# Three kinds of SBUF pools give back their space tile by tile instead of pool by pool

## The chip, the cores and the metric

The kernel runs on one core of one Trainium2 chip. The metric is the device time of one execution in microseconds (us); the median of three runs is given. Beside it stands one profiled execution with its own time, from which all rows of the trace are taken.

The engines are called PE (TensorE, matmul), DVE (VectorE), ACT (ScalarE), POOL (GpSimd) and SP (SyncE, which here only issues loads and stores). DMAs are issued on three queues: SP's, ACT's and POOL's.

## What is computed

Two layers of a transformer over 512 latent tokens and 256 context tokens of width 1024, all in float32. Layer 0 mixes tokens by neighbourhood attention (8 heads) beside a spatial gating unit (SGU), layer 1 by retention (8 heads). Each is followed by a gated MLP with a depthwise convolution (ConvFFN). Around every part stand RMS norms, and shift, scale and gate come from a conditioning vector through `ada_w`. Only the latent stream is put out.

```python
for i in range(DEPTH):                      # DEPTH = 2
    sh1, sc1, g1, sh2, sc2, g2 = jnp.split(silu(c) @ ada_w[i] + ada_b[i], 6)
    h_lat = modulate(rmsnorm(x, norm_g[i, 0]), sh1, sc1)
    h_ctx = modulate(rmsnorm(xc, norm_g[i, 0]), csh1, csc1)
    y = hybrid_na_sgu(h_ctx, h_lat, ...) if i % 2 == 0 else retention_mixer(h_ctx, h_lat, ...)
    x = x + g1 * rmsnorm(y_lat, norm_g[i, 1])
    h = modulate(rmsnorm(x, norm_g[i, 2]), sh2, sc2)
    x = x + g2 * rmsnorm(conv_ffn(h, ...), norm_g[i, 3])
    # in layer 0 the context stream xc goes the same way, with csh, csc, cg
```

## The kernel before

The work stands as one stream of instructions for each engine, which a tile framework records from the Python program; it assigns addresses to tiles and adds the semaphore waits that the tiles' uses demand. Within an engine the order is that of the program; engines run apart and meet only at waits. One helper (L71) records every operation of PE, DVE and ACT, so rows of the trace are told apart by the names of tiles, not by lines.

A float32 product is made of three matmuls of a split operand: ACT writes the high part, DVE the low part (`split`, L110). So every weight is loaded by SP into one of three `raw` buffers, split by ACT and then by DVE, and used by PE. A `raw` buffer is free again when DVE has done its part.

There are five phases one after the other, and each opens its own pool of SBUF space with `phase` (L138): `sguw` (the SGU), `attp` (attention), `ffnp0` (the first ConvFFN), `retp` (retention) and `ffnp1` (the second ConvFFN). Inside the SGU two more are opened: `firstp` for the first norms (L751) and `sgup` (L791), which takes over `firstp`'s space. A phase's pool lies where the one before it lay. `lay` (L145) fixes the place of each tag in a pool. The pools that live through the whole program (`cp`, `bp`, `lp`, and those in PSUM and DRAM) are opened elsewhere.

Since a phase's tiles lie on those of the phase before, the first instructions that write them must wait for the old uses. In the kernel before, the framework lets a pool's space go as a whole: the first write into the new pool on an engine waits for the last uses, by every engine and DMA queue, of all tiles of the old pool.

What else the prediction names:

- Attention adds bias tiles to its scores. `load_slab` (L988) loads a strip of the bias table with a DMA on POOL's queue, `bias_tiles` (L993) scales it on POOL (L998) and adds it to `mask` (L1003 to L1005), which SP loads at the phase's start. POOL also copies one half of `kb` (L970), the low part of the keys, which PE reads in `s<-kb,q`.
- `ada_half` (L251) works out the gates and scales in small steps between the other work: a memset of `acc` on POOL (L257), a row load into it (L258), four loads of `ar`, and multiply-adds of `ar` into `acc` on DVE. The steps stand at fixed places of the program.
- `mx` and `wsg` are products of the SGU on PE, `wsg` its last ones.
- At each phase's end the residual of every token tile is stored to DRAM from ACT's queue (`xd`, L390), normed and transposed on PE (`ht`, `htc`), scaled into `sa` and `sb` (or `hc`) and split into `hb` (or `h0c`, `h1c`) for the next phase.
- In a ConvFFN `wp` and `wpm` are the first two blocks' weights, `pf` their products, `cw` the convolution's weights, `f0..`, `f1..` and `fo..` weights of later blocks, `pre`, `cv`, `b12` and `blk` work tiles.
- In retention `rv` holds the values, `rn` is their product in PSUM, `dist`, `cos`, `sin`, `dec` and `gng` are tables, `rwv`, `rwg`, `rwk` and `wx` weights, `rkc` and `rq` products.

Of the kernel before, what the change touches and what calls it, by code (L numbers as in the profile page):

```python
# [78 lines left out]
class Trunk:  # L79
# [56 lines left out]
        return self.place(i, name, at)  # L136

    def phase(self, ctx, name, extra, wide=2048):  # L138
        self.xp = ctx.enter_context(self.tc.tile_pool(name=name, bufs=1))
        self.extra = extra  # L140
        self.wide = wide
        self.turn = 0
        return self.xp
# [581 lines left out]
    def sgu(self, y, xn):  # L725
        S, V, T, G, a = self.S, self.V, self.T, self.G, self.a
        toks = (4, 5, 0, 1, 2, 3)
        with ExitStack() as ctx:
# [5 lines left out]
            def ug_units(which, js):  # L734
                return [
                    self.unit(
                        a["hyb_ug"][(which * 4 + i) * P : (which * 4 + i + 1) * P], f"ug{which}{i}", at=0 if which else Q3
                    )
                    for i in js
                ]  # L740

            def ug(ps, t, w, ks, cs=slice(0, 512)):
                hc = self.hcols(t)
                for k in ks:
                    c = slice((k % 2) * 512 + cs.start, (k % 2) * 512 + cs.stop)
                    wk = w[k // 2 % len(w)]
                    self.mm3(ps, hc(k), (wk[0][:, c], wk[1][:, c]), k == 0, k == KD - 1)

            ps = {}
            with ExitStack() as c2:  # L750
                fp = c2.enter_context(self.tc.tile_pool(name="firstp", bufs=1))  # L751
                cs = self.cs
                c4 = fp.tile([P, KD, 4], F32R, name="c4", tag="c4")
                for s in range(2):
                    S.activation(c4[:, :, 2 * s], cs[:, 8 * s : 8 * s + 8], AF.Copy)
                    V.tensor_tensor(
                        out=c4[:, :, 2 * s + 1],
                        in0=cs[:, 8 * s : 8 * s + 8],
                        in1=c4[:, :, 2 * s].bitcast(F32),
                        op=ALU.subtract,  # L760
                    )
                self.c4 = c4
                self.alloc_h("a")
                xT = {}
                ada = self.ada_first(0, fp, True, "C")
                chunks = ((2, (4, 5)), (0, (0, 1)), (1, (2, 3)))
                for n, (chunk, ct) in enumerate(chunks):
                    if n:
                        self.first_load(ct, xn)
                    self.first_x(ct, xn)  # L770
                    for _ in range((1, 2, 5)[n]):
                        next(ada, None)
                    self.first_xT(chunk, ct, xn, fp, xT)
                for _ in ada:
                    pass
                for q in range(4):
                    w = ug_units(1, (q,))
                    for chunk, ct in chunks:
                        self.first_h(q, chunk, xT)
                    if q < 3:  # L780
                        ada = self.ada_first(q + 1, fp, q == 0, "B")
                    for n, t in enumerate(toks):
                        if q == 0:
                            ps[t] = self.ps(f"ug1{t}", "C" if t > 3 else "A")
                        if q < 3:
                            ug(ps[t], t, w, (2 * q, 2 * q + 1))
                        if n < 4:
                            next(ada, None)
                    for _ in ada:
                        pass  # L790
            sp = ctx.enter_context(self.tc.tile_pool(name="sgup", bufs=1))  # L791
            self.lay(sp, [("sT0", 3072), ("sT1", 3072), ("un0", 1536), ("un1", 1536), ("vnh", 3072), ("vnl", 3072)])
            u = [sp.tile([P, 6, 256], F32, name=f"un{i}", tag=f"un{i}") for i in range(2)]
            vh = sp.tile([P, 6, 512], F32R, name="vnh", tag="vnh")
# [1180 lines left out]
```

## Time and profile before

| what | value |
| --- | --- |
| median of 3 runs | 1856.94 us (1853.55 to 1860.03) |
| profiled execution, its own time | 1852.3 us |
| its span, first to last instruction | 1850.5 us |
| mean granted clock of PE | 0.990 |
| busy: PE, DVE, ACT, POOL | 96%, 75%, 56%, 18% |
| moved by DMA | 253.45 MB |

The span is counted from the first instruction of the program, and all times of rows are from its start. In a timeline's row stand the start, the time (of several merged instructions together), the engine, line, operation, the tile written and those read, the sizes and the count; in square brackets is how long the engine had sat idle before it, and what ended that. An engine with "q" is its queue: there the row is the issue of a DMA. The places where one phase gives way to the next lie, for PE, near 97 us (`sgup`), 158 us (attention), 395 to 415 us (first ConvFFN), 941 to 960 us (retention) and 1474 to 1499 us (second ConvFFN).

### The profile page before, as it was taken

The numbers are of one execution on the slowest core, as the hardware profiler recorded it, in microseconds if no ns is written. First come the engines' busy times: TensorE is split into PE (matmuls) and PEld (weight loads), VectorE is DVE, ScalarE is ACT, GpSimd is POOL, SyncE is SP. The second block draws the span as 40 slices with busy tenths as digits, with TensorE's granted clock in tenths as the row PEclk, the third lists the DMA queues.
The fourth block names the chain that finished last, engine by engine and source line by source line (L and its number), as shares of the span: only waits on it lengthen the run. The fifth ranks groups of instructions, "written<-read, shape, count | busy, mean of one in ns | idle before, by whom it ended". The sixth has DMA issues, their size and how long they took to land. (4 is left out here: it accounts for less than half of the span.)

```text
span 1850.5 us, 28777 instructions
## 1 busy us (share of the span) xinstructions
PE 1781.8 (96%) x10928; PEld 1582.7 (86%) x10928; DVE 1391.1 (75%) x2347; ACT 1029.3 (56%) x1866; POOL 330.0 (18%) x462
## 2 busy tenths in 40 slices
PE   7999899999999999999999999999999889999997
PEld 4888777679998899998888988988999789989996
DVE  4877675789878788787866676676656699988886
ACT  6533455677555565564664534344434467766763
POOL 1102122131122322222112011011101100222221
PEclk9999999999999999999999999999999989999999
DMA  7344321155577777786722422331321225877762
GB/s 297 112 141 143 117 82 36 55 171 148 178 156 168 174 175 161 156 173 151 265 97 92 143 99 80 125 113 58 105 69 60 101 82 157 215 197 201 171 161 97
DMA packets 84399, 253.45 MB, mean 137 GB/s; under 512 B 11026, under 2 KB 11538, under 8 KB 84260
## 3 DMA queue, kind: packets, MB, share of 16 engines
q1 hardware_dynamic: 55044, 191.27, 30.9%
q0 software_dynamic: 26912, 51.95, 16.4%
q10 hardware_dynamic: 2304, 8.39, 1.1%
q8 instruction: 86, 1.41, 0.3%
q14 instruction: 53, 0.43, 0.1%
HBM read 191.80 MB, written 39.85 MB: 125 GB/s over the span
## 5 line engine op out<-in xcount | busy, mean ns | idle before, releaser
L71 DVE SCALAR_TENSOR_TENSOR acc<-ar,cs,acc 128x512 f32<-128x512 f32 x256 | 185.7, 751 | 33.7 <-DMA ar<-in_adaw 24.7
L71 DVE SCALAR_TENSOR_TENSOR cv<-pre,cw,cv 128x769 f32<-128x769 f32 (+1 forms) x176 | 153.6, 884 | 4.9 <-ACT cv L71 4.2
L71 PE MATMUL rn<-rwv,h0c 128*128 128x256 f32 x768 | 136.3, 281 | 3.0 <-ACT h0c L71 3.0
L71 PEld LDWEIGHTS rn<-rwv,h0c 128*128 128x128 f32 x768 | 118.2, 191 | 3.7 <-ACT h0c L71 3.4
L71 PE MATMUL wf<-fo,g 128*128 128x512 f32 x432 | 112.6, 394 | 0.5 <-DVE fo L71 0.5
L71 PE MATMUL rn<-rwv,h1c 128*128 128x256 f32 x384 | 108.1, 282 | 0.4 <-DVE h1c L71 0.2
L1688 POOL DMA_DIRECT2D yf<-yp x64 | 55.1, 861 | 257.0 <-ACT yp L71 233.8
L71 ACT ACTIVATE cv<-pre,cw 128x770 f32<-128x770 f32 (+1 forms) x88 | 81.3, 925 | 24.0 <-DVE pre L71 23.4
L71 PE MATMUL rn<-rwg,h0c 128*128 128x256 f32 x512 | 90.0, 280 | 0.0
L71 PEld LDWEIGHTS wf<-fo,g 128*128 128x128 f32 x432 | 75.9, 188 | 13.8 <-DVE fo L71 1.4
L71 PE MATMUL px<-hs,wc 128*128 128x384 f32 (+1 forms) x480 | 79.3, 314 | 5.4 <-ACT pre L71 3.2
L71 PEld LDWEIGHTS px<-hs,wc 128*128 128x128 f32 x480 | 74.3, 191 | 10.8 <-ACT pre L71 5.4
L71 ACT ACTIVATE pre<-px 128x256 f32<-128x256 f32 (+2 forms) x160 | 54.3, 367 | 47.7 <-PE px L71 47.6
L71 ACT COPY yp<-wf 128x512 f32<-128x512 f32 x118 | 67.8, 576 | 19.0 <-PE wf L71 16.5
L71 PEld LDWEIGHTS rn<-rwg,h0c 128*128 128x128 f32 x512 | 78.1, 189 | 0.0
L71 PE MATMUL pz<-hb,wa 128*128 128x384 f32 (+1 forms) x480 | 77.3, 308 | 0.0
L71 PE MATMUL px<-hb,wa 128*128 128x384 f32 (+1 forms) x480 | 77.1, 308 | 0.0
L71 PE MATMUL py<-blk,wb 128*128 128x384 f32 (+1 forms) x480 | 76.9, 308 | 0.0
L71 PE MATMUL px<-blk,wb 128*128 128x384 f32 (+1 forms) x480 | 76.7, 309 | 0.0
L71 PEld LDWEIGHTS px<-hb,wa 128*128 128x128 f32 x480 | 73.2, 188 | 3.2
L71 PEld LDWEIGHTS px<-blk,wb 128*128 128x128 f32 x480 | 73.4, 189 | 3.0 <-ACT pre L71 0.2
L71 PEld LDWEIGHTS rn<-rwv,h1c 128*128 128x128 f32 x384 | 72.9, 190 | 1.5 <-DVE h1c L71 1.3
(1272 smaller groups left out, 5112.6 us busy)
## 6 DMA issues: line engine op xcount, KB each, us to landing
ar<-in_adaw SPq DMA_DIRECT2D x96, 512.0 KB, 3.9
yf<-yp POOLq DMA_DIRECT2D x64, 256.0 KB, 4.2
yd<-yp POOLq DMA_DIRECT2D x54, 256.0 KB, 5.0
yd<-ypg POOLq DMA_DIRECT2D x54, 256.0 KB, 4.9
fin<-xd SPq DMA_DIRECT2D x8, 512.0 KB
xn<-in_x SPq DMA_DIRECT2D x6, 512.0 KB, 4.6
xb<-in_x SPq DMA_DIRECT2D x6, 512.0 KB
xd<-xb ACTq DMA_DIRECT2D x6, 512.0 KB, 2.8
```

The source lines that it names most:

```text
L71: i = f(*args, **kw)
L1688: G.dma_start((yd[t] if first else y[t])[:, o], v, accum_op=ALU.add)
```

## The change

Three pools are opened with `reuse_waits="tile"`: those of the five phases, of the first norms and of the SGU. With it the framework lets their space go tile by tile: a write waits for the uses of those old tiles that lie under the written tile itself, and for no others. What is computed, the tiles, their places and the order of the instructions on each engine stay as they were.

```diff
     def phase(self, ctx, name, extra, wide=2048):
-        self.xp = ctx.enter_context(self.tc.tile_pool(name=name, bufs=1))
+        self.xp = ctx.enter_context(self.tc.tile_pool(name=name, bufs=1, reuse_waits="tile"))
         self.extra = extra
...
             with ExitStack() as c2:
-                fp = c2.enter_context(self.tc.tile_pool(name="firstp", bufs=1))
+                fp = c2.enter_context(self.tc.tile_pool(name="firstp", bufs=1, reuse_waits="tile"))
                 cs = self.cs
...
-            sp = ctx.enter_context(self.tc.tile_pool(name="sgup", bufs=1))
+            sp = ctx.enter_context(self.tc.tile_pool(name="sgup", bufs=1, reuse_waits="tile"))
             self.lay(sp, [("sT0", 3072), ("sT1", 3072), ("un0", 1536), ("un1", 1536), ("vnh", 3072), ("vnl", 3072)])
```

The waits of the instructions change in some fifty places. In the rows below the square brackets name the semaphores that an instruction waits for: one for each engine (PE, DVE, Activation, Pool), eight for DMAs issued on SP and ACT (DMAHW0 to 7) and eight for those issued on POOL (DMASW0 to 7). How far each must have counted does not stand there.

SP's queue at the start of attention, where the mask is loaded among the weights of the first projection:

```order
 L97 DMA acc_1559<-in_adab_row 1x512 [waits DMAHW4_49,DMAHW2_49,Pool_49]
 L97 DMA wk0r<-in_hyb_qkv 128x1024 [waits DMAHW6_49,DVE_49]
-L97 DMA mask<-in_mask 128x768 [waits PE_49]
+L97 DMA mask<-in_mask 128x768
 L97 DMA wv0r<-in_hyb_qkv 128x1024 [waits DMAHW1_49,DVE_49]
 L97 DMA ar_1699<-in_adaw 128x1024 [waits DMAHW7_49,DVE_49]
```

The mask's load waited for PE's last product of the SGU and now waits for nothing of its own. On POOL, at the same place, the first `slab` load waits for PE in both kernels, but for another count: 800 before, which is the last `wsg` product, and 632 now, which is the last `mx` product. The wait for later products of the SGU has moved behind it, to the bias tiles and to the copy of `kb`:

```order
 L991 DMA slab_1656<-in_rpb 128x1x256 [waits PE_49]
 L998 TENSOR_SCALAR slab_1656<-slab_1656 128x256 [waits DMASW0_49]
-L1003 TENSOR_TENSOR tm_1905<-slab_1656,mask 128x256 [waits DMAHW4_49,Pool_49]
+L1003 TENSOR_TENSOR tm_1905<-slab_1656,mask 128x256 [waits DMAHW4_49,PE_49,Pool_49]
 L1003 TENSOR_TENSOR tm_1905<-slab_1656,mask 128x256
 L1004 TENSOR_TENSOR tm_1905<-slab_1656,mask 128x128
```

At the start of retention and of the second ConvFFN it is ACT, DVE, PE and SP whose waits change. For SP at retention's start:

```order
 L97 DMA rwg01r<-in_ret_vg 128x1024 [waits DVE_49]
-L97 DMA dist<-in_dist 128x778 [waits DMAHW3_49,DMAHW4_49,DMAHW2_49,DMAHW5_49,DMAHW0_49,DMAHW6_49,DVE_49,DMAHW7_49,PE_49,Activation_49]
-L97 DMA cos<-in_cos 128x512
-L97 DMA sin<-in_sin 128x512
-L97 DMA dec<-in_decay 128x16
-L97 DMA gng<-in_gn_col 128x16
-L97 DMA ar_9587<-in_adaw 128x1024 [waits DVE_49]
+L97 DMA dist<-in_dist 128x778 [waits DMAHW3_49,PE_49]
+L97 DMA cos<-in_cos 128x512 [waits DMAHW4_49]
+L97 DMA sin<-in_sin 128x512 [waits DMAHW5_49]
+L97 DMA dec<-in_decay 128x16 [waits DMAHW6_49]
+L97 DMA gng<-in_gn_col 128x16 [waits DMAHW7_49]
```

The five tables waited for the last uses of the whole first ConvFFN, the last store of `xd` (DMAHW2) among them; each now waits for the older tile under it. In the same way ACT's first write of `rv` no longer waits for that store, while DVE's write of `rv` and ACT's later split of `rwg` do. In the second ConvFFN ACT's split of `wp` waited for the last store of `xd` and now waits only for its own load; DVE and PE, which follow with `wp` and its product `pf`, lose their lists in the same way (PE's from eleven semaphores to one), and the wait for the store has gone to `b12`. In the first ConvFFN the same holds for `wpm`, with `blk` in the place of `b12`.

## The prediction

> **What bounds the kernel now.** I read the page first, then the idle time of TensorE (PE) along the whole span, then the timeline of each engine around the five places where a pool gives way to the next.
>
> ```profile
> PE 1781.8 (96%) x10928; PEld 1582.7 (86%) x10928; DVE 1391.1 (75%) x2347; ACT 1029.3 (56%) x1866; POOL 330.0 (18%) x462
> ```
>
> PE is busy for 96% of the span, and its idle time is the span's 1850.5 less 1781.8, 69 us with both ends. So waits removed from the other engines pay only where PE itself stands still, or runs at half the granted clock behind a longer gap. The longest gap is 7.10 us, at the start of the attention phase; its PE row says that the GpSimd (POOL) copy of `kb` ended it.
>
> ```profile
> 151.33 0.53 POOL L257 MEMSET acc<- 128x512 f32 x1 [1.52 <-DVE al L71]
> 158.62 0.86 POOL L991 DMA_DIRECT2D slab<-in_rpb  x1 [6.76 <-PE wsg L71]
> ```
>
> ```profile
> 166.60 1.72 POOL L1003 TENSOR_TENSOR tm<-slab,mask 128x256 f32<-128x256 f32 x2
> ```
>
> ```profile
> 180.75 0.63 POOL L991 DMA_DIRECT2D slab<-in_rpb  x1 [0.30 <-POOL tm L1005]
> ```
>
> ```profile
> 184.50 0.98 POOL L257 MEMSET acc<- 128x512 f32 x2
> 190.09 1.93 POOL L970 CAST kb<-kb 64x768 fp32r<-64x768 f32 x1 [4.61 <-DVE kb L71]
> ```
>
> ```profile
> 156.81 0.33 SPq L97 DMA_DIRECT2D wk0r<-in_hyb_qkv  x1
> 158.33 0.33 SPq L97 DMA_DIRECT2D mask<-in_mask  x1
> ```
>
> ```profile
> 185.40 0.33 SPq L97 DMA_DIRECT2D ar<-in_adaw  x1
> ```
>
> ```profile
> 182.49 0.63 DVE L71 TENSOR_TENSOR kb<-pk,ka 64x448 fp32r<-64x448 f32 x1 [0.39 <-ACT ka L71]
> 188.75 0.75 DVE L71 SCALAR_TENSOR_TENSOR acc<-ar,cs,acc 128x512 f32<-128x512 f32 x1 [5.63 <-DMA ar<-in_adaw]
> 189.53 0.42 DVE L71 TENSOR_TENSOR kb<-px,ka 64x256 fp32r<-64x256 f32 x1
> ```
>
> ```profile
> 192.07 0.58 PE L71 MATMUL s<-kb,q 128*128 128x256 f32 x1 [7.10 <-POOL kb L970]
> ```
>
> Read backwards, PE waited for POOL's cast, this for VectorE's (DVE's) `kb`, this stood behind an `acc` step that sat 5.63 us for the load of `ar`, and SyncE (SP) issued that load behind a row load into `acc`, which the memset of 184.50 lets go. The memset stands on POOL behind three `slab` loads and two rounds of bias tiles, and the first of these sat 6.76 us for the last product of the SGU. So a pool's wait at 158 us is paid by PE at 185.
>
> **Attention's start, the main term.** The first `slab` load now waits for an earlier count of PE, that of the last `mx` product:
>
> ```profile
> 117.30 0.34 PE L71 MATMUL mx<-vnh,sguw 128*128 128x384 f32 x1
> ```
>
> It can go as soon as POOL has done the memset that ends at 151.86, near 152. The mask's load has no wait left and follows `wk0r` on SP: 157.1 instead of 158.33. Their landings:
>
> ```profile
> DMA to landing us min/median/max: 3.2/4.3/7.4
> ```
>
> ```profile
> ar<-in_adaw SPq DMA_DIRECT2D x96, 512.0 KB, 3.9
> ```
>
> The first line is of `slab`. Even at 7.4 it is there by 159.4 and scaled by 159.8. The mask is smaller than an `ar` load; with that one's 3.9 it is there at 161.0, and so the first bias tile starts at 161.1 instead of 166.60, 5.5 us earlier. (It also waits for the SGU's products now, done by 158.3.) POOL's next steps follow each other, so the third `slab` load goes at 175.25. It took 3.2 us on a quiet queue; moved ahead it runs beside a projection weight, so I take the median 4.3 and keep 4.4 of the 5.5. The memsets come at 180.1, the `ar` load at 181.0, the `acc` step at 184.35 (DVE is free at 183.12), the cast at 185.7 and PE's product at 187.67. **Gain 4.4 us**; what is late next is the mask's load and then the same `ar` load. Bounds: 1.3 if the third `slab` takes 7.4; 5.6 if the `acc` step need not wait at all, which is DVE's own limit.
>
> **The clock behind that gap.** The stretches are those in which the granted clock changes:
>
> ```profile
> 183.25:186.66 3.41, 1.73 (x15) 1.00 0.08 29
> 186.66:190.07 3.41, 0.00 (x0) 1.00 0.35 128
> 190.07:193.49 3.42, 1.42 (x5) 0.50 0.30 62
> 193.49:196.90 3.41, 3.41 (x10) 0.50 0.64 238
> 196.90:200.31 3.41, 3.41 (x17) 1.00 0.38 136
> ```
>
> ```profile
> 637.22:640.63 3.41, 1.64 (x8) 1.02 (x7) 3.41 (x5) 1.07 (x3) 0.00 (x0) 1.00 0.57 159
> 640.63:644.05 3.42, 3.42 (x11) 2.92 (x10) 3.42 (x7) 2.65 (x4) 1.22 (x2) 0.50 0.88 208
> ```
>
> The columns are the stretch, its length, PE's busy time and count (in the second fence also of the weight loads, DVE, ScalarE and POOL), then the clock and the DMA share. A full stretch does 17 matmuls at clock 1.00 and 10 at 0.50, so a halved one loses 3.41 x 7/17 = 1.4 us, and the 1.42 us of the stretch before it another 0.6: 2.0 in all. A stretch with 1.73 us of work kept the clock, one with 1.64 lost half of it. A remaining gap of 2.7 us would here lie in two stretches (1.68 and 1.0) and halve nothing; were it in one, 0.7 of work would be left and the clock would drop. Where the stretches begin, no execution chooses. I take half: **gain 1.0** (0 to 2.0).
>
> The Trainium skill (TensorE: Matmul & The Clock Gate, section "HAM oscillation — how this bites in real kernels") has as its rule that no PE gap beyond some 3.4 us should occur; by it the remaining 2.7 us are harmless, all 2.0 are gained, and the sum below would be 7.8. The stretch at 637.22, which lost its clock with 1.77 us idle, speaks against it.
>
> **Retention's start.**
>
> ```profile
> 943.28 3.41 DMA xd<-fin
> ```
>
> ```profile
> 947.10 0.60 ACT L71 ACTIVATE rv<-rn 128x512 fp32r<-128x512 f32 x1 [0.96 <-DMA xd<-fin]
> ```
>
> ```profile
> 941.84 0.33 SPq L97 DMA_DIRECT2D rwg01r<-in_ret_vg  x1
> 946.94 0.33 SPq L97 DMA_DIRECT2D dist<-in_dist  x1
> ```
>
> ```profile
> 949.16 0.69 DVE L71 TENSOR_TENSOR h1c<-hc,h0c 128x512 fp32r<-128x512 f32 x1 [0.74 <-ACT h0c L71]
> ```
>
> ScalarE's (ACT's) `rv` copy no longer waits for the store of `xd`: 0.96 us earlier, and with it the half of `h` that PE needs. But DVE's `rv` now waits for that store by itself, ahead of `h1c`, and SP's tables (`dist`, `cos`, `sin`, `dec`, `gng`) go at 942.2 instead of 946.94, beside the store. If it still takes 3.41, the gain is 0.96; if 5.29, as the store in the fence below, which had loads beside it, DVE's `rv` starts at 948.6 and `h1c` at 949.2, no gain. I take **0**, since it is nearest to that row. Lower bound: at 7.4 (the slowest `slab`) the loss is 2.2. The tables themselves gain nothing, since they are read much later.
>
> **The last ConvFFN's start.**
>
> ```profile
> 1488.28 5.29 DMA xd<-xd
> 1493.75 1.07 ACT wp L71
> 1494.84 1.23 DVE wp L71
> 1496.07 1.28 DVE sb L71 x4
> ```
>
> ```profile
> 1494.27 0.27 PE L71 MATMUL ht<-ident,yr 128*128 128x128 f32 x1
> 1494.91 0.47 PE L71 MATMUL pf<-hb,wp 128*128 128x256 f32 x2 [0.36 <-issue]
> 1496.12 1.10 PE L71 MATMUL pf<-hb,wp 128*128 128x256 f32 x7 [0.74 <-DVE wp L71]
> ```
>
> This is the chain of waits: store, ACT's `wp` split, DVE's. `wp` now waits for its own load alone and runs some 2.9 us earlier on ACT, so DVE has it by 1493.2. DVE's next step, `sb`, needs PE's transpose that ends at 1494.54, so DVE gains 1496.07 - 1494.6 = 1.4 us. PE loses the 0.74, the 0.36 in front of an instruction with eleven waits, and what lies around them, and then follows DVE, whose rows are closed up from here: **gain 1.4** (1.1, the two idle times alone, to 1.6, a start straight after the transpose). `b12` now takes over the wait for the store, at 1494.7 at the earliest, after the landing at 1493.57.
>
> **Costed at nothing.** At the first ConvFFN's start the same kind of wait goes from ACT:
>
> ```profile
> 412.46 0.63 ACT L71 ACTIVATE wpm<-f011r 128x512 fp32r<-128x512 f32 x1 [1.44 <-DVE t L71]
> ```
>
> ```profile
> L71 PE MATMUL pf<-hb,wpm 128*128 128x384 f32 x24 | 4.4, 338 | 0.0
> ```
>
> PE's products of `wpm` (second line; the last column is its idle time) follow others without a gap, and these hide it; without that cover it would be worth up to 1.44. SP's early `cw` and `f012r` are read later, by steps that PE does not wait for in this stretch. The waits taken from `mx` and `rq` had long been met, and the few added ones name transfers and products of the phase before.
>
> **Sum.** 4.4 + 1.0 + 0 + 1.4 = 6.8 us. From the profiled execution's 1852.3 that gives 1845.5. That execution lay 4.6 below the median of the runs, 1856.94; the same 6.8 from the median gives 1850.1, which I forecast. Most of PE's later work follows without slack, so I expect the gain to last to the end.
>
> **Rivals.** (1) Every cover holds: 5.6 + 2.0 + 0.96 + 1.6 = 10.2, 1846.7. For it: the `ar` load is the only thing DVE sat for. Against: two more transfers must be quick. (2) The wait moves to the transfers: the third `slab` takes 7.4 in the crowd and the clock is halved all the same, 1.3 + 1.4 = 2.7, 1854.2. For it: the first `slab` took that long, beside the same kind of loads. Against: the others took 3.2 and 4.3. (3) Slower: the early tables crowd out the store at retention's start. Between 941.84 and the landing, 512 KB of weight, 512 KB of store and 0.7 MB of tables would be under way; served at the chip's mean of 137 GB/s in this profile, with the store last, it lands at 954.5 instead of 946.69. `h1c` is then 6.0 us late on DVE and PE's gap brings one more halved stretch, 1.4: 7.4 lost. That gives 1850.1 + 7.4 = 1857.5, slower than before; the point from which it decides is a landing at about 954, or about 950 with attention's gains at their lower bounds.
>
> ```profile
> DMA packets 84399, 253.45 MB, mean 137 GB/s; under 512 B 11026, under 2 KB 11538, under 8 KB 84260
> ```
>
> With those bounds (1.3 and 1.4 gained, 7.4 lost) the time is 1861.6. Against it: ACT's queue had a store done in 3.41 beside a whole weight load. The Trainium skill (DMA: Bandwidth & Descriptors, section "Issuing engines are not separate DMA queues") says that transfers issued by different engines run on the same 16 DMA engines and interleave; by it the store is neither last nor untouched. This speaks for a store of 5 us, and the sum stays.
>
> **How the numbers follow.** A measurement of this kernel can tell about 0.3%, 5.6 us, from no change: faster is below 1851.4, slower above 1862.5. The forecast has 0.54, of it 0.42 faster and 0.12 within, since its own range, 1847 to 1854, crosses that line. Rival 1 has 0.22, faster. Rival 2 has 0.14, 0.02 faster and 0.12 within. Rival 3 has 0.10, 0.08 slower (with whatever else a crowded queue brings) and 0.02 within. Together 0.66, 0.26 and 0.08. The range, 1842 to 1858, reaches from rival 1, less the spread of the runs, past rival 2 to no change.
>
> **What would show it.** In attention: the first `slab` near 152, the first bias tile near 161, the memset pair near 180, `ar` near 181, and PE's gap before `s<-kb,q` at 1.5 to 3 us instead of 7.1, with clock 1.00 or one halved stretch behind it. At retention: `rv` on ACT without its 0.96, the tables near 942, and the store's landing, which decides that term. At the last ConvFFN: ACT's `wp` near 2.9 us earlier beside the rows around it, and no idle time of PE before `pf<-hb,wp`. I am wrong if PE's gap in attention stays above 6 us, if the store lands more than 6 us after its issue, or if gaps of the same size open up later in the phases and take the gain back.

## The result and the profile after

| | before | after |
|---|---|---|
| median of four runs, us | 1856.61 (1853.55 to 1860.03) | 1847.61 (1846.31 to 1850.15) |
| profiled execution, us | 1852.3 | 1846.42 |
| its span, us | 1850.5 | 1844.6 |
| mean granted clock | 0.990 | 0.989 |
| PE's idle time before `s<-kb,q`, us | 7.10 | 1.73 |
| the last store `xd<-fin`, issue to landing, us | 3.41 | 6.70 |

The ratio is 0.9953, 95% interval 0.9931 to 0.9974: the change makes the kernel faster by some half a per cent, 9.0 us by the medians and 5.9 by the two profiled spans.

**Attention's start.** The timeline of the changed kernel, POOL first, then SP, DVE and PE:

```profile
151.21 0.86 POOL L991 DMA_DIRECT2D slab<-in_rpb  x1
160.94 2.69 POOL L1003 TENSOR_TENSOR tm<-slab,mask 128x256 f32<-128x256 f32 x2 [5.16 <-DMA mask<-in_mask]
174.25 0.63 POOL L991 DMA_DIRECT2D slab<-in_rpb  x1 [0.30 <-POOL tm L1005]
178.22 0.99 POOL L257 MEMSET acc<- 128x512 f32 x2
184.13 1.90 POOL L970 CAST kb<-kb 64x768 fp32r<-64x768 f32 x1 [4.92 <-DVE kb L71]
```

```profile
156.71 0.43 SPq L97 DMA_DIRECT2D mask<-in_mask  x1
179.12 0.33 SPq L97 DMA_DIRECT2D ar<-in_adaw  x1
```

```profile
182.76 0.75 DVE L71 SCALAR_TENSOR_TENSOR acc<-ar,cs,acc 128x512 f32<-128x512 f32 x1 [4.07 <-DMA ar<-in_adaw]
```

```profile
186.09 0.39 PE L71 MATMUL s<-kb,q 128*128 128x256 f32 x1 [1.73 <-POOL kb L970]
```

The same chain as before, 6 us earlier. POOL's first `slab` goes as soon as POOL is free; the bias tile `tm` now waits 5.16 us for the mask, and DVE still waits 4.07 us for `ar`. The stretches of the granted clock there (PE's busy time follows the length; the clock stands after the five engines):

```profile
182.96:186.37 3.41, 1.69 (x14) 1.48 (x13) 3.28 (x6) 1.48 (x5) 1.90 (x1) 1.00 0.00 0
186.37:189.79 3.42, 3.42 (x11) 2.74 (x11) 2.46 (x5) 3.19 (x7) 1.95 (x1) 0.50 0.73 205
189.79:193.20 3.41, 3.41 (x17) 2.79 (x16) 3.38 (x8) 0.78 (x1) 0.00 (x0) 1.00 0.34 118
```

One stretch is halved instead of two.

**Retention's start** went against me. SP, the chain of waits, DVE and PE:

```profile
935.21 0.38 SPq L97 DMA_DIRECT2D dist<-in_dist  x1
937.06 0.50 SPq L97 DMA_DIRECT2D gng<-in_gn_col  x1
```

```profile
936.22 6.70 DMA xd<-fin
```

```profile
943.24 0.69 DVE L71 TENSOR_TENSOR rv<-rn,rv 128x512 fp32r<-128x512 f32 x1 [3.65 <-DMA xd<-fin]
943.85 0.68 DVE L71 TENSOR_TENSOR h1c<-hc,h0c 128x512 fp32r<-128x512 f32 x1
```

```profile
941.04 0.80 PE L71 MATMUL rn<-rwv,h0c 128*128 128x256 f32 x2 [1.06 <-ACT h0c L71]
944.59 0.58 PE L71 MATMUL rn<-rwv,h1c 128*128 128x256 f32 x1 [2.75 <-DVE h1c L71]
```

The tables' five loads are issued between 935.21 and 937.06, around the store; the store takes 6.70 us; DVE's `rv` sits 3.65 us for it, and `h1c`, which PE needs, stands behind `rv`. PE's gap before `h0c` shrinks to 1.06, as ACT's `rv` no longer waits, but a new one of 2.75 opens behind it. Before the change PE had this one gap there:

```profile
949.18 0.80 PE L71 MATMUL rn<-rwv,h0c 128*128 128x256 f32 x2 [2.14 <-ACT h0c L71]
```

From one product (`rkc`) to another (`rq`) behind that place, before and now:

```profile
943.03:960.00 16.97, 13.70 (x87) 12.42 (x86) 9.70 (x15) 12.26 (x22) 2.34 (x4) 0.80 0.62 197
935.99:955.44 19.45, 14.51 (x88) 13.16 (x86) 9.58 (x15) 12.35 (x22) 2.38 (x4) 0.74 0.51 172
```

The length less PE's busy time is its idle time: 4.94 us now and 3.27 before. The other part of the 2.5 us is the clock, which is halved in three stretches now and in two before.

**The last ConvFFN's start.** DVE's split of `wp`, and PE:

```profile
1487.31 1.23 DVE L71 TENSOR_TENSOR wp<-f111r,wp 128x1024 fp32r<-128x1024 f32 x1 [0.58 <-ACT wp L71]
1490.48 1.37 DVE L71 TENSOR_SCALAR sb<-ht,ab 128x128 f32<-128x128 f32 x4 [1.94 <-PE ht L71]
```

```profile
1490.19 3.12 PE L71 MATMUL pf<-hb,wp 128*128 128x256 f32 x24
```

`wp` is ready at 1488.54, 1.9 us before `sb` starts, and PE's `pf` rows run on without idle time.

**Where the time went.** The end of a span mixes all places. So I compare the start of one and the same product of PE in two profiles: its start in the kernel before less its start in the other is the other's lead there, in us. The first row gives the start before; the labels are those of the experiments below.

| | 183 | 200 | 560 | 700 | 943 | 960 | 1494 | 1525 | end |
|---|---|---|---|---|---|---|---|---|---|
| the change | 0.6 | 6.7 | 7.1 | 7.6 | 7.1 | 4.6 | 4.1 | 6.0 | 5.9 |
| e1_attn_only | -0.3 | 7.9 | 7.9 | 8.1 | 8.9 | 8.4 | 7.7 | 7.8 | 10.0 |
| e2_no_attn | 0.5 | 2.8 | 2.6 | 4.0 | 3.3 | 2.4 | 2.0 | 3.3 | 3.6 |
| e3_no_ret | 0.8 | 5.4 | 5.8 | 8.1 | 9.0 | 7.9 | 5.2 | 6.5 | 5.1 |
| e4_ret_only | -0.5 | -0.3 | 0.0 | -2.6 | -2.3 | -3.6 | -6.2 | -6.2 | -5.6 |
| e5_tables_behind | -0.4 | 7.0 | 7.1 | 5.8 | 6.4 | 7.0 | 5.4 | 6.6 | 5.8 |
| e6_both_under | -0.6 | 6.9 | 7.1 | 7.9 | 7.0 | 8.0 | 7.7 | 9.8 | 8.7 |
| e7_rv_clear | -0.8 | 5.1 | 5.1 | 7.8 | 5.2 | 4.0 | 1.6 | 2.8 | 3.5 |
| e8_mask_pool | -1.0 | 8.7 | 8.0 | 7.8 | 4.3 | 2.5 | 1.3 | 2.5 | 2.3 |
| e9_both | -1.0 | 8.6 | 8.2 | 4.1 | 4.2 | 5.9 | 2.4 | 3.9 | 2.1 |
| e10_change | -2.2 | 3.8 | 3.7 | -0.4 | -1.6 | -2.9 | -3.0 | -1.0 | -2.7 |
| e11_spare | -1.3 | 7.9 | 7.3 | 6.6 | 1.7 | 1.4 | -1.8 | -0.2 | -0.9 |
| e12_repair | -0.1 | 5.6 | 5.4 | 5.1 | 5.1 | 4.6 | 1.7 | 3.0 | 3.8 |

Read it by steps, not by its last column. For the change: 6.0 from 183 to 200 (attention), 2.5 lost from 943 to 960 (retention), 1.9 won from 1494 to 1525 (the last ConvFFN). Row e10 is the same program once more, on another chip: the steps are 6.0, -1.3 and 2.0, though its end is 2.7 behind. It was 2.2 late before attention and lost 4.1 between 560 and 700, where the instructions and their waits are those of the change: PE idled 5.8 us there, 3.4 in the kernel before and 2.9 in the change, and two stretches were halved instead of one.

### The profile page after: what moved, and what is told of

It is laid out like the page before. It is cut to its first block, busy times and chain, and to the rows that moved or that the text cites. A ratio compares the mean times of both kernels' runs of the same rounds, so it can differ in the third digit from the quotient of the medians.

```text
span 1844.6 us, 28733 instructions
## 1 busy us (share of the span) xinstructions
PE 1781.6 (97%) x10928; PEld 1584.6 (86%) x10928; DVE 1391.5 (75%) x2347; ACT 1030.8 (56%) x1866; POOL 329.3 (18%) x462
## 4 chain that ended last, share of the span: by engine, by line
PE 36%; DVE 7%; DMA 3%; ACT 2%; issue 1%; POOL 1%; DVEq 0%; POOLq 0%; ACTq 0%
PE rn L71 11%; PE px L71 4%; PE wf L71 3%; PE wr L71 3%; PE rq L71 2%; PE py L71 2%; PE rk L71 2%; DVE cv L71 1%; PE pz L71 1%; PE rkc L71 1%; PE ro L71 1%; PE rx L71 1%; PE wf1C L71 1%; PE wf1A L71 1%; PE pf L71 1%
```

## Experiments: which pool brings what

Each kernel is timed beside the kernel before on the same chip; the ratios below are to that, with 95% intervals. In the first four only the condition differs; e1 and e4 also leave the first norms' and the SGU's pool as before.

```
+        by_tile = {"reuse_waits": "tile"} if name == "attp" else {}     # e1
+        by_tile = {"reuse_waits": "tile"} if name != "attp" else {}     # e2
+        by_tile = {"reuse_waits": "tile"} if name != "retp" else {}     # e3
+        by_tile = {"reuse_waits": "tile"} if name == "retp" else {}     # e4
-        self.xp = ctx.enter_context(self.tc.tile_pool(name=name, bufs=1, reuse_waits="tile"))
+        self.xp = ctx.enter_context(self.tc.tile_pool(name=name, bufs=1, **by_tile))
```

**e1, attention's pool alone.**

> The pool of attention alone waits tile by tile; all others as before. Theory A (attention brings the whole gain; retention's start gives some of it back): PE's idle time before `s<-kb,q` 7.10 -> about 1.7 us, PE from 196 us on 6 to 7 us ahead of the kernel before, no idle time of 2.75 before `rn<-rwv,h1c` at retention's start, the store `xd<-fin` there lands some 3.4 us after its issue as before, and the lead of about 7 us stays to the end: profiled execution near 1845.3, ratio to before near 0.996, 1 us faster than the whole change or level with it. Rival B (what retention's start loses comes from arriving there early, not from its own pool): the 2.75 us appear here too and the lead falls to 4, profiled near 1848, ratio 0.998. Rival C (each pool brings a share): the lead is under 4 us already at 250 us.

Median 1844.40 against 1853.15, ratio 0.9950 (0.9933 to 0.9968). PE at attention's start and DVE at retention's:

```profile
186.48 0.38 PE L71 MATMUL s<-kb,q 128*128 128x256 f32 x1 [1.24 <-POOL kb L971]
```

```profile
938.77 0.69 DVE L71 TENSOR_TENSOR rv<-rn,rv 128x512 fp32r<-128x512 f32 x1 [1.01 <-ACT rv L71]
```

The gap falls to 1.24 and no stretch of the clock is halved behind it, so the step is 8.1 us. DVE's `rv` waits for ACT, as before the change, and the store lands 3.33 us after its issue (in this and the following numbers of that kind: from ACT's issue to the last of the store's completions in the trace). Attention's pool alone gives as much as the whole change; theory A holds, B and C fall.

**e2, all pools but attention's.**

> Every pool but attention's waits tile by tile. Theory A: PE's 7.10 us before `s<-kb,q` stay, but for 0.6 us gained before them; retention's start loses 2 to 3 us by the store that lands about 7 us after its issue, the last ConvFFN's start gains 1 to 1.5 us; the sum is 0 to 1 us slower than before, profiled 1852 to 1853.5, ratio 1.000 to 1.0006. Rival B (the loss depends on when retention starts against other transfers): no loss there, 1.5 to 2 us faster, ratio 0.999. Rival C (each pool brings a share): 2.5 us or more faster, ratio under 0.9987.

Median 1853.34, ratio 0.9999 (0.9985 to 1.0013). The store lands after 6.55 us and PE's gap before `h1c` is 2.60; the last ConvFFN brings 1.3. The sum is nothing by the median, as theory A said; the profiled execution, 3.6 us ahead at its end, is the fastest of twelve. One thing theory A had not foreseen: PE's gap at attention is 5.24 instead of 7.10, with attention's waits as before. The timelines of POOL show where most of it comes from, the same small bias tile before and in e2 (whose line numbers are one higher):

```profile
168.28 1.50 POOL L1004 TENSOR_TENSOR tm<-slab,mask 128x128 f32<-128x128 f32 x1
```

```profile
167.32 0.52 POOL L1005 TENSOR_TENSOR tm<-slab,mask 128x128 f32<-128x128 f32 x1
```

Two rounds of bias tiles took 8.83 us before and 6.77 in e2. So the length of this step does not follow from its waits alone; what DVE runs beside it seems to come into it too (last section).

**e3, all pools but retention's.**

> Every pool but retention's waits tile by tile. Theory A: the lead of about 7 us that the whole change had at 880 us stays through retention's start (no 2.75 us before `rn<-rwv,h1c`, the store lands in about 3.4 us), and the last ConvFFN adds 1 to 1.5: lead at the end 8 to 8.7 us, profiled near 1843.8, 2.6 us faster than the whole change, ratio to before near 0.9953 if the whole change is at 0.9968 by its profile. Rival B (the loss at retention's start is not of its pool): as the whole change, profiled near 1846.4.

Median 1847.10, ratio 0.9961 (0.9943 to 0.9979). The loss at retention's start is gone as far as the new gap goes: the store lands in 3.22 and no gap over 0.4 us precedes `h1c`, while the one before `h0c`, 1.95, is the old one. But the time is no better than that of e1, and attention won 4.6 instead of 6.0, since the second `slab` with its scaling took 1.6 us longer than in the change (164.52 to 171.24 against 164.91 to 170.01, from its issue to its first `tm`):

```profile
187.58 0.58 PE L71 MATMUL s<-kb,q 128*128 128x256 f32 x1 [3.43 <-POOL kb L971]
```

The 2.6 us that theory A expected over the whole change can't be seen in the medians.

**e4, retention's pool alone.**

> Retention's pool alone waits tile by tile. Theory A: nothing changes up to 940 us; there the tables' loads are issued some 7 us after the weight's instead of behind the store, the store lands about 7 us after its issue instead of 3.4, DVE's `rv<-rn,rv` waits for it, and PE idles 2.75 us more before `rn<-rwv,h1c`: 2 to 3.5 us slower, profiled 1854.5 to 1855.8, ratio 1.0011 to 1.0019. Rival B (the crowd of transfers comes only with the earlier arrival from attention): no difference, ratio 1.000. Rival C (the forecast's term): 0, between 2.2 slower and 1.0 faster.

Median 1853.62 against 1853.15, ratio 1.0007 (0.9994 to 1.0020): no verdict by itself, between A and B. The place gives it. SP, DVE and PE:

```profile
944.56 0.38 SPq L97 DMA_DIRECT2D dist<-in_dist  x1
```

```profile
952.32 0.69 DVE L71 TENSOR_TENSOR rv<-rn,rv 128x512 fp32r<-128x512 f32 x1 [3.38 <-DMA dec<-in_decay]
```

```profile
953.66 0.58 PE L71 MATMUL rn<-rwv,h1c 128*128 128x256 f32 x1 [2.77 <-DVE h1c L71]
```

Retention starts here as late as before, and the 2.77 us are there all the same; theory B falls. The view puts DVE's wait down to `dec`, which landed at about the same time. DVE's `rv` has no `dec` among its waits, but it has the semaphore of the store, which was issued at 945.57 and landed 6.43 us later, at 952.00.

## Experiments: the two halves of retention's loss

The tiles of retention's pool lie over those of the first ConvFFN: `rv1`, `rg` and the weights over `fin`, out of which the last `xd` is stored. `rv1` waits for every reader of `fin`, the last store too. Three layouts, each on top of the whole change:

```
-            order = [("dist", ND), ("cos", 512), ("sin", 512), ("dec", 16), ("gng", 16), (None, 24)]
-            order += [("rv0", 1536), ("rv1", 1536), ("rg", 1024), ("w3", SLOT), ("w4", SLOT), ("w5", SLOT)]
-            order += [("e0", ND), ("e1", ND), (None, 16), ("rk0", 512), ("rk1", 512), (None, 48), ("rq0", 512), ("rq1", 512)]
```

With `tables` for the first of these lines and `rest` for the last, e5 has

```
+            order = [("rv0", 1536), ("rv1", 1536)] + tables
+            order += [("rg", 1024), ("w3", SLOT), ("w4", SLOT), ("w5", SLOT)] + rest
```

so that `cos` and the tables behind it lie over `fin`, and `dist` and `rv` do not; e6 has

```
+            order = [("rv0", 1536), ("rg", 1024), ("rk0", 512), ("rk1", 512)] + tables
+            order += [("rv1", 1536), ("w3", SLOT), ("w4", SLOT), ("w5", SLOT)]
+            order += [("e0", ND), ("e1", ND), (None, 16), (None, 48), ("rq0", 512), ("rq1", 512)]
```

so that all tables and `rv1` lie over it; and e7 has

```
+            order = [("rv0", 1536), ("rv1", 1536), ("rg", 1024), ("w3", SLOT), ("w4", SLOT), ("w5", SLOT)]
+            order += [("e0", ND), ("e1", ND), (None, 16), ("rk0", 512), ("rk1", 512), (None, 48), ("rq0", 512)]
+            order += tables + [("rq1", 512)]
```

so that neither does.

**e5, most tables behind the store, `rv` clear of it.**

> The whole change, and in retention's pool `rv0` and `rv1` change places with the tables, so that `rv` lies clear of `fin` and the loads of `cos`, `sin`, `dec` and `gng` wait for the last store `xd<-fin` (`dist` alone is still early). Theory A (the loss at retention's start needs both: a store made slow by the early tables, and `rv` lying over `fin`, so that DVE waits for that store): the store lands 3.4 to 4.5 us after its issue, DVE's `rv<-rn,rv` follows ACT's within 0.2 us, no idle time of 2.75 before `rn<-rwv,h1c`; the lead over the kernel before at the first `rn<-rwv,h1c` behind it is as large as just ahead of it or larger, 2.5 to 3.5 us more than in the whole change: profiled near 1843, ratio to before 0.994 where the whole change stands at 0.9953. Rival B (the loss comes with retention's early weights and steps, whatever the tables do): the 2.75 stay.

**e6, tables and `rv1` both behind the store.**

> The whole change, and in retention's pool the tables and `rv1` both lie under `fin`, so that the loads of all five tables and DVE's `rv<-rn,rv` wait for the last store `xd<-fin`. Theory A (the early tables slow the store): the store lands about 3.4 us after its issue as in the kernel before, `rv` on DVE waits little (under 0.5 us), PE's idle time before `rn<-rwv,h1c` is under 0.3 us, and the lead stays, 2.5 us more than in the whole change behind that place. Rival B (the store is slow for another reason, the weight `rwg01r` or where it comes in time): it lands 6 to 7 us after its issue, `rv` waits 3 us and more, the gap of about 2.7 us stays, the same lead as the whole change.

**e7, `rv` clear, tables early.**

> The whole change, and in retention's pool `rv0` and `rv1` lie clear of `fin` while the tables' loads stay as early as in the whole change. Theory A (the store's lateness costs time only by DVE's wait): the store still lands about 7 us after its issue, DVE's `rv<-rn,rv` follows ACT's within 0.2 us, PE's gap before `rn<-rwv,h1c` is gone, the lead 2.5 us more than in the whole change behind it. Rival B (the crowd of transfers delays something else as well, as the weight `rwg00r` or `rwg01r` on ACT): a gap of 1 us or more turns up within 10 us behind that place, and 1 us or less is won.

DVE's `rv` in e5, e6 and e7:

```profile
940.26 0.69 DVE L71 TENSOR_TENSOR rv<-rn,rv 128x512 fp32r<-128x512 f32 x1
```

```profile
940.12 0.69 DVE L71 TENSOR_TENSOR rv<-rn,rv 128x512 fp32r<-128x512 f32 x1 [0.51 <-DMA xd<-fin]
```

```profile
941.50 0.69 DVE L71 TENSOR_TENSOR rv<-rn,rv 128x512 fp32r<-128x512 f32 x1
```

| | store, issue to landing | PE's largest gaps before `h0c`, `h1c` | 943 to 960 | PE's idle time there | ratio |
|---|---|---|---|---|---|
| the change | 6.70 | 1.06, 2.75 | -2.5 | 4.9 | 0.9953 |
| e5 | 4.01 | 1.06, 0.23 | +0.6 | 2.2 | 0.9946 (0.9927 to 0.9966) |
| e6 | 3.59 | 1.06, 0.53 | +1.0 | 3.0 | 0.9942 (0.9923 to 0.9961) |
| e7 | 6.98 | 1.06, 0.22 | -1.2 | 2.6 | 0.9943 (0.9922 to 0.9965) |

With the tables behind it the store is quick, and then it does no harm that `rv1` lies under it (e6): the tables' early loads make the store slow. With the tables early it stays slow, and with `rv` clear the gap is gone all the same (e7): the loss needs `rv` over `fin` as well. So theory A is shown in both halves.

The step from 943 to 960 is a poorer witness than PE's idle time, since it holds the clock's chances too: e1 and e3, whose retention pool is as before, have steps of -0.5 and -1.1. Of the idle time between the same two products there are 3.2 to 3.7 us with the pool as before (before, e1, e3), 4.8 to 5.0 with it as in the change (the change, e2, e4, e8, e10), and 2.2 to 3.0 with one of these layouts (e5, e6, e7, e9, e11, e12). The gain did not reach the end everywhere: e5's profiled execution took 1846.5 us, where some 1843 were expected.

In e7 something of rival B is there too: ACT's split of the weight `rwg`, whose tile also lies over `fin`, waits for the store, and `h0c` and PE wait 0.47 us behind it:

```profile
945.24 1.06 ACT L71 ACTIVATE rwg<-rwg00r 128x1024 fp32r<-128x1024 f32 x1 [0.89 <-DVE h1c L71]
946.21 0.61 ACT L71 ACTIVATE h0c<-hc 128x512 fp32r<-128x512 f32 x1
```

The store landed at 945.10 there; that the view names `h1c` is the same confusion as in e4. And e7 lost its lead to three halved stretches in a row, behind one in which PE had idled 1.40 us.

## Experiments: what is late next in attention

**e8, the mask on POOL's queue**, on top of the whole change.

```
-            self.load(self.mask, a["mask"])
+            self.G.dma_start(self.mask, a["mask"])
```

> The whole change, and attention's mask is loaded on the POOL queue just ahead of the first `slab` instead of on SP behind the weights. Theory A (after the change the mask is what POOL's bias tiles wait for, and through them the memsets, the `ar` load and DVE): the first `tm` starts near 156 instead of 160.94, the memset pair near 173.5 instead of 178.22, `ar` is issued near 174.5, DVE's 4.07 us of waiting for it go, and PE's idle time before `s<-kb,q` falls from 1.73 to under 0.6 us with no halved clock behind it: 1.2 to 3 us more lead at 197 us than the whole change. Rival B (the transfers or DVE's own queue are the limit, not the mask): the gap stays between 1.2 and 3.4 us. Rival C: `slab`'s load falls behind the mask's on POOL and is late by as much as the mask was; the gap grows.

Median 1849.57 against 1854.54, ratio 0.9970 (0.9955 to 0.9985). POOL and PE:

```profile
157.96 3.01 POOL L1003 TENSOR_TENSOR tm<-slab,mask 128x256 f32<-128x256 f32 x2
177.96 0.99 POOL L257 MEMSET acc<- 128x512 f32 x2
```

```profile
185.77 0.28 PE L71 MATMUL s<-kb,q 128*128 128x256 f32 x1
```

Half of theory A came: the first `tm` is 3 us earlier though this execution was 1.6 late by then, PE has no gap at all, and 183 to 200 brings 9.6 us instead of 6.0. But the memset pair comes only 0.26 earlier, not 4.7: from the first `tm` to the memsets it takes 20.0 us instead of 17.3, with both rounds of bias tiles (4.5 and 4.4 instead of 3.8 and 4.0) and both `slab` loads slower. And the median is not better.

**e9, both repairs** (e6's layout and the mask on POOL), and **e10, the whole change again**, on one chip.

> The whole change with both repairs: retention's tables and `rv1` under `fin` (as in the run before that kept the store at its old pace) and attention's mask on the POOL queue. Theory A (each removes its own wait and the two add up): no idle time before `s<-kb,q`, no 2.7 us before `rn<-rwv,h1c`; 1.5 us from the first and 2.5 from the second over the whole change on the same chip, less or more by 2 us with the number of halved stretches: median 2 to 5 us below the whole change's, ratio to before 0.993. Rival B (what attention's mask wins is given back by the clock and by gaps in the first ConvFFN, as the single execution of that kernel seemed to show): the lead that is there at 197 us, 8 us and more, is down to 6 at 940 us, and the median is level with the whole change's.

> The whole change once more, on the same chip as the run with both repairs. Theory A: ratio to before 0.994 to 0.997; in its profile the store at retention's start lands about 7 us after its issue and PE's gap of about 2.7 us before `rn<-rwv,h1c` is there again, since it follows from which tile lies over which, while the gap before `s<-kb,q`, which hangs on three transfers, comes out anywhere between 1.2 and 3.5 us. Rival B (the gap at retention's start was a chance of one execution): it is under 1 us here.

e9: 1849.39 against 1856.68, ratio 0.9962 (0.9945 to 0.9979). e10: 1852.43, ratio 0.9978 (0.9962 to 0.9994), above the 0.994 to 0.997 expected. Both local effects of e9 are there: 9.6 us at attention, DVE's `rv` waiting 0.49 us for a store that landed after 3.56, +1.7 from 943 to 960. They do not add up in the time: the lead falls from 8.2 at 560 us to 4.1 at 700. In e10 the gap at retention's start is there again, so it was no chance:

```profile
952.82 0.58 PE L71 MATMUL rn<-rwv,h1c 128*128 128x256 f32 x1 [2.60 <-DVE h1c L71]
```

**e11, both repairs and a spare load**, and **e12, retention's repair alone again**, on one chip. Was the mask's gain given back because every later transfer of SP and ACT takes the next semaphore when one leaves SP's queue?

```
-            order += [("sst", 8, 4), (None, 16), ("xk0", 1024), ("kb0", 768), ("xk1", 1024), ("kb1", 768)]
+            order += [("sst", 8, 4), ("spare", 16), ("xk0", 1024), ("kb0", 768), ("xk1", 1024), ("kb1", 768)]
...
+            self.load(ap.tile([P, 16], F32, name="spare", tag="spare")[:1], a["mask"][0:1, 0:16])
```

> Both repairs as before (retention's tables and `rv1` under `fin`; the mask on POOL), and a load of 64 bytes into 16 unused columns on SP in the mask's old place among the weights, so that every later transfer of SP and ACT keeps the semaphore that it has in the whole change. Theory A (what the mask on POOL wins in attention, 3.6 us by the start times of PE's products, was given back because the numbering of all later transfers moved by one): the lead won between 183 and 200 us is about 9.6 us and is still there at 940; the median is 3 us and more below that of retention's repair alone, run beside it on the same chip, ratio to before near 0.992. Rival B (it is given back by the clock and by gaps of the first ConvFFN that differ from run to run, or by nothing that this load touches): the median is level with retention's repair alone within 2 us, or above it.

> The whole change with retention's repair alone (the tables and `rv1` under `fin`), once more, on the same chip as the run with both repairs and the spare load. Theory A: ratio to before 0.993 to 0.996, the store at retention's start lands about 3.5 us after its issue, PE has no gap over 1.1 us between the `rn` products there, and the lead won in attention lies between 4.6 and 8.1 us, as in the other kernels with these waits. Rival B (the low median of its first run was chance): 0.997 or more.

e11: 1846.42 against 1856.34, ratio 0.9954 (0.9936 to 0.9971). e12: 1847.85, ratio 0.9958 (0.9945 to 0.9972). They are level, so the numbering is not it: theory A falls. In e11 the lead of 7.9 at 200 us was 1.7 at 943.

Taken together: retention's repair without the mask (e5, e6, e7, e12) has ratios of 0.9946, 0.9942, 0.9943 and 0.9958, mean 0.9947; the whole change has 0.9953 and 0.9978, mean 0.9966. This points to some 3 us for the repair, while the steps from 943 to 960 of the same kernels differ by 1.9 on average and PE's idle time there by 2.2; no single pair of intervals parts them. The mask on POOL (0.9970, 0.9962, 0.9954) is not shown to help. No kernel here is shown to beat the change.

## Why the prediction came out as it did

The forecast was 1850.1, between 1842 and 1858 and faster; the median is 1847.61. The sum was 6.8; the second measurement, 0.9978, is 4.2 us, so the two lie on either side of it. By the places, the profiled executions gained 5.4 (6.0 - 2.5 + 1.9) and 6.7 (6.0 - 1.3 + 2.0): that 6.8 lies so near is in part luck, since what attention gave beyond its term hides what retention lost.

- **Attention's start, 4.4 and 1.0 for the clock.** Mechanism right, size too small: 6.0 instead of 5.4, in both executions of the change. Of this the gap gave 5.4 (7.10 to 1.73) instead of 4.4, and the clock 0.6 (1.4 us lost instead of 2.0) instead of 1.0. The worked times were close at first (`tm` at 161.1, measured 160.94) and then too late: the `s<-kb,q` product was put at 187.67 and came at 186.09. Of these 1.6 us, 0.8 are the two rounds of bias tiles and the `slab` between (13.3 us from the first `tm` to the third `slab`, where I moved the 14.15 of before unchanged), 0.9 the third `slab` (I took the median landing of 4.3), 0.2 the start, and the `ar` load took 0.3 back. The gap is paid once more by the clock, which the forecast had left open: one stretch halved, two before. What I named as late next, the mask and then `ar`, was late next. My upper bound had held DVE to its old place, free at 183.12; it was free at 178.69, as the split of `wv` ran at 164.37 instead of 167.93.
- **Retention's start, 0.** This step failed. I took the store at 5.29 us, from the row of a store that had loads beside it; it took 6.70 in the change, and 6.3 to 7.0 wherever the tables were early, beyond the 6 us that I had named as the sign of being wrong here. With 6.70 in the same working DVE's `rv` starts at 950.0 and `h1c` at 950.6 instead of 949.16, a loss of 1.4; PE's idle time grew by 1.7. With the clock 2.5 us were lost in the profiled execution, beyond my bound of 2.2, and 0.9 to 2.5 in the five executions with retention's pool as in the change. Rival 3 described the mechanism rightly (early tables, the store, DVE's `rv`, `h1c`) and priced it far too high: it let the store land last of all, at 954.5, which is 11.2 us after its issue.
- **The last ConvFFN's start, 1.4.** Right: 1.9 and 2.0 in the change, 1.1 to 2.1 in all kernels that have it, and 0.1 and 0.0 in e1 and e4, which have not. The clock is in this too: with two halved stretches near 1515, as before, it is 1.1 to 1.5, and 1.6 to 2.1 in the four profiles with only one (the change, e6, e10, e11).
- **Costed at nothing.** From 200 to 560 us, across the first ConvFFN's start, the lead moves by 0.4 in the change and by 0.7 at most in any kernel. Right.
- **The gain lasts to the end.** Only on average. Between the places of the change the lead of single executions falls by up to 4.9 us (e11, 700 to 943) and grows by up to 2.7 (e7, 560 to 700), and this, not the sum, sets the last digits.

## What to carry to other kernels

Letting a pool go tile by tile pays where the first instruction of the new phase stands at the head of a long chain; price that chain by each of its own links, since a link's duration changes with what it now runs beside. Where it frees loads that nobody needs yet, ask which transfer they will share the wires with, and which tile lies over that transfer's source: loads that came too early cost more here, a gap of 2.75 us, than the old wait they came out of, which had made a gap 1.08 us longer. If a place loses, lay the early loads and the first tiles anew before giving up the change; a layout moves waits as surely as code does.

## What the runs showed of the hardware

**Half a stretch of idle time halves the clock.** In the 14 profiles I counted the 3.41 us stretches at full clock by PE's idle time in them, without the last ones of each program. With 1.77 us and more, 78 of 81 were followed by a halved one; with 1.60 to 1.77, 5 of 17; with 1.2 to 1.6, 3 of 57. Two stretches of the changed kernel lie on either side, with 1.65 and 1.66 us of PE's work:

```profile
937.30:940.72 3.42, 1.65 (x10) 1.03 (x8) 1.09 (x2) 3.39 (x8) 0.56 (x1) 1.00 0.89 280
940.72:944.13 3.41, 0.80 (x2) 0.50 (x2) 0.89 (x2) 2.79 (x4) 0.00 (x0) 0.50 0.36 127
```

```profile
991.92:995.33 3.41, 1.66 (x9) 1.01 (x7) 2.09 (x4) 1.34 (x3) 0.00 (x0) 1.00 0.86 308
995.33:998.74 3.41, 3.12 (x25) 2.83 (x24) 3.41 (x9) 2.92 (x3) 0.00 (x0) 1.00 0.61 202
```

So a gap of some 2 us costs 1.4 more or nothing, by where the stretches begin, and each profile has 6 to 10 gaps of 1.6 us and more. This is one reason for leads that move by several us where the program is the same, and gaps that differ in length are the other (e10 above); it was counted, not tested. The Trainium skill (TensorE: Matmul & The Clock Gate, section "HAM oscillation — how this bites in real kernels") asks for no PE gap beyond some 3.4 us; here one gap of 1.73 us was enough, and the measurement decides.

**POOL and DVE are slow beside each other.** A bias tile of 128x128 on POOL takes from 0.52 to 1.53 us; in all seven rows of 1.50 and more, DVE was busy throughout. DVE's split of `wk` beside `tm` took 1.94 us in the change, and 1.23 before, where no `tm` ran with it. Of these splits of `wq`, `wk` and `wv` in the 14 profiles, the 88 with POOL idle took 1.21 to 1.23 us, and the 46 beside more than 0.8 us of POOL's work 1.21 to 1.95:

```profile
160.95 1.94 DVE L71 TENSOR_TENSOR wk<-wk0r,wk 128x1024 fp32r<-128x1024 f32 x1 [1.61 <-ACT wk L71]
```

```profile
161.21 1.23 DVE L71 TENSOR_TENSOR wk<-wk0r,wk 128x1024 fp32r<-128x1024 f32 x1 [1.25 <-ACT wk L71]
```

The Trainium skill (GPSIMD Engine Reference, section "1. Specifications") says that POOL shares its SBUF interfaces with VectorE and contends with DVE instructions that have two SBUF inputs; these rows agree, and no run was made to test it alone.
